# S5 branch of an encoder layer: products and sums moved from GpSimd to VectorE, plain copies moved to ScalarE

## Chip, cores and metric

The kernel runs on one core of one Trainium2 chip. The metric is the device time of one execution, in microseconds (us). Three executions of the kernel before took 2364.59, 2369.57 and 2371.45 us; their median is 2369.57 us.

## What is computed

One encoder layer on 1024 tokens of width 1024, in float32:

```
x = LN1(alpha*x + 0.5*SwiGLU_1(x))
x = LN2(alpha*x + W_out(g_A*W_oA(MLA(x)) + g_B*W_oB(S5(x))))
x = LN3(alpha*x + 0.5*SwiGLU_2(x))
x = LN4(alpha*x + sigmoid(x W_pg) * (p W_pp))
```

The change lies in the S5 branch, a bidirectional linear scan over 32 groups of 16 channels with 64 complex states each, once forward and once backward in time:

```
lam_bar = exp(lam*dt);  b_bar = ((lam_bar - 1)/lam) * b
bu = einsum(u, b_bar);  xs[t] = lam_bar*xs[t-1] + bu[t]     (or reversed)
y  = Re(einsum(xs, c)) forward + the same backward + d*u
z  = gelu(y);  S5 = z * sigmoid(z @ w_glu)
```

## The kernel before

TensorE computes float32 products as three products of a high and a low part each, so nearly every weight tile is first split: ScalarE copies the high part out (`split`, line 64), VectorE subtracts it from the raw tile (line 65). A slab of weights of 128 x 1024 takes 48 products of 128x512; the tiles of the high and low part have three buffers each.

The S5 branch (`s5_branch`, line 1032) is a generator. Its first part (to line 1247) makes tables from the parameters: powers of lam_bar (`PV`, `PW`), the tables `T1` and `T2` of the rotation angles, `br`, `bi` (b_bar) and the zeroed `bd` tiles. The tables T1 and T2 are made on GpSimd. Then come 8 steps, t = 0 to 7, of four groups each. Partitions 0 to 63 (`fw`) hold the forward direction, 64 to 127 (`bw`) the backward one.

- `gen(t)` (line 1249) makes the operands of step t: V = PV*c and W = PW*b_bar, both complex products of six 128x512 operations on VectorE (`cmul`, line 1139), with one more to negate the imaginary part of V (line 1263); four transposes each of W's parts (`pw`, line 1270) and their copies out of PSUM (`WTr`, `WTi`, line 1272); four copies of 64x64 into the block-diagonal `bd` (line 1278); the short kernel K from the products `pkx` (line 1283), which goes through DRAM into the Toeplitz tile M (lines 1292 and 1295); and C, S = T2*T1 (`Cw`, `Sw`, six operations on GpSimd, line 1298).
- `scan(t, ops)` (line 1302) makes the block sums `pe` on TensorE (line 1311), turns them by C and S (four products on VectorE, two sums on GpSimd), scans them over 128 blocks (`tensor_tensor_scan`, line 1327), and turns them back: four products on VectorE, then four half-width differences or sums, the forward halves on GpSimd (line 1335) and the backward halves, which are stored reversed, on VectorE (line 1336). The result is X, two tiles.
- `read_out(t, ops, X)` (line 1339) sums M, V and X into `py` on TensorE (lines 1344 and 1346), applies gelu (`zo`) and stores.

The main program calls the generator step by step (lines 767 to 773). Between two steps it issues two slabs of the projection that makes the gates (`project`, products `pg` at line 84), one slab after step 0. The program is placed by a scheduler that knows dependencies and estimated durations: it sets the order on each engine, so that products `pg` lie between the branch's own. Each engine works its own list in order. The projection of the latents with its root mean squares (`latents`, line 562, products `pms`) runs just ahead of step 0; part of it is on GpSimd (lines 591 to 594).

Of the kernel before, what the change touches and what calls it, by code (L numbers as in the profile page):

```python
# [24 lines left out]
AF = mybir.ActivationFunctionType  # L25
# [20 lines left out]
def layer_kernel(ctx, tc, A):  # L46
# [712 lines left out]
    sp = pool(left, "s5")  # L759
    s5p = pool(left, "s5p")  # L760
    step = s5_branch(tc, A, ud, zd, sp, s5p, dram, pdn, idt)
    next(step)
    project(sp, us[:2], state)
# [268 lines left out]
def s5_branch(tc, A, ud, zd, keep, pool, dram, pdn, idt):  # L1032
# [11 lines left out]
    V, S, G, PE = nc.vector, nc.scalar, nc.gpsimd, nc.tensor  # L1044
    MUL, ADD, SUB = ALU.mult, ALU.add, ALU.subtract

    def tile(shape, tag, bufs=1, dt=F32):
        return pool.tile([128] + shape, dt, tag=tag, bufs=bufs, name=tag)

    def load(name, shape):  # L1050
        t = tile(shape, name)
        nc.sync.dma_start(t, A[name])
        return t
# [3 lines left out]
    def t32(name):  # L1057
        if name not in slots:
            if not room:
                t = tile([16, 32], ("t2", "t3", "Xr")[len(slots) // 16])  # L1060
                room.extend(t[:, i, :] for i in range(16))
            slots[name] = room.pop()
        return slots[name]

    def tt(out, a, b, op, eng=G):
        eng.tensor_tensor(out=out, in0=a, in1=b, op=op)

    def ts(out, a, s1, op0, s2=None, op1=None, eng=G):
        if op1 is None:
            eng.tensor_scalar(out=out, in0=a, scalar1=s1, scalar2=None, op0=op0)  # L1070
        else:
            eng.tensor_scalar(out=out, in0=a, scalar1=s1, scalar2=s2, op0=op0, op1=op1)
# [31 lines left out]
    q, r, p, z = t32("q"), t32("r"), t32("p"), t32("z")  # L1104
# [34 lines left out]
    def cmul(outr, outi, a, b, tmp, eng=G):  # L1139
        tt(outr, a[0], b[0], MUL, eng)  # L1140
        tt(tmp, a[1], b[1], MUL, eng)
        tt(outr, outr, tmp, SUB, eng)
        tt(outi, a[0], b[1], MUL, eng)
        tt(tmp, a[1], b[0], MUL, eng)
        tt(outi, outi, tmp, ADD, eng)

    cr, ci = load("c_re", [32, 16]), load("c_im", [32, 16])
    br, bi = tile([32, 16], "bb_re"), tile([32, 16], "bb_im")
    PV = [tile([32, 8], f"PV{i}") for i in range(2)]
    PW = [tile([32, 8], f"PW{i}") for i in range(2)]  # L1150
    T1, T2 = (tile([32, 16], "T1r"), tile([32, 16], "T1i")), (tile([32, 8], "T2r"), tile([32, 8], "T2i"))
# [38 lines left out]
    def tmp(n, eng=G):  # L1190
        return bigs[eng][:, :, 0:n]

    rb = (tile([32, 16], "Vr", 2), tile([32, 16], "Vi", 2))
    nc.sync.dma_start(rb[0], A["b_re"])
    nc.sync.dma_start(rb[1], A["b_im"])
# [12 lines left out]
    fw, bw = slice(0, 64), slice(64, 128)  # L1208
# [40 lines left out]
    def gen(t):  # L1249

        ss = slice(4 * t, 4 * t + 4)
        B4 = [128, 4, 8, 16]

        def x(a):
            return a[:, ss, :, None].to_broadcast(B4)

        def y(a):
            return a[:, ss, None, :].to_broadcast(B4)

        g1, g2 = tile([4, 8, 16], "v1"), tile([4, 8, 16], "v2")  # L1260
        Vr, Vi = tile([4, 8, 16], "Vr", 2), tile([4, 8, 16], "Vi", 2)
        cmul(Vr, Vi, (x(PV[0]), x(PV[1])), (y(cr), y(ci)), g1, V)
        V.tensor_scalar(out=Vi, in0=Vi, scalar1=-1.0, scalar2=None, op0=MUL)
        Wr, Wi = tile([4, 8, 16], "Wr"), tile([4, 8, 16], "Wi")
        cmul(Wr, Wi, (x(PW[0]), x(PW[1])), (y(br), y(bi)), g1, V)
        WT = []
        for w, tag in ((Wr, "WTr"), (Wi, "WTi")):
            ps = pdn.tile([128, 512], F32, tag="dn", name="pw")
            for s in range(4):
                PE.transpose(ps[:, s * 128:s * 128 + 128], w[:, s].rearrange("p a b -> p (a b)"), idt)  # L1270
            o = tile([4, 128], tag, 2)
            S.activation(o, ps.rearrange("p (s n) -> p s n", s=4), AF.Copy)
            WT.append(o)
        Vf = [v.rearrange("p s a b -> p s (a b)") for v in (Vr, Vi)]

        for src, o in zip((br, bi), bd):
            for d, r in enumerate((fw, bw)):
                V.tensor_copy(o[r, :, 64 * d:64 * d + 16], src[r, ss, :])
        bz = [o.rearrange("p g x -> p (g x)") for o in bd]
        pk = pdn.tile([128, 512], F32, tag="dn", name="pkx")  # L1280
        for g in range(4):
            for i in range(2):
                PE.matmul(pk[:, 0:128], lhsT=bz[i][:, 112 * g:112 * g + 128], rhs=Vf[i][:, g, :],
                          start=(g == 0 and i == 0), stop=(g == 3 and i == 1))
        K = tile([240], "K")
        S.activation(K[fw, 0:128], pk[bw, 0:128], AF.Copy)
        S.activation(K[fw, 128:240], pk[fw, 16:128], AF.Copy)
        c = slice(112, 128)
        tt(K[0:64, c], K[0:64, c], pk[0:64, 0:16], ADD, V)
        V.scalar_tensor_tensor(out=K[0:64, c], in0=eye[0:64, :], scalar=dsk[0:64, t:t + 1], in1=K[0:64, c],  # L1290
                               op0=MUL, op1=ADD)
        nc.sync.dma_start(kd[t], K[0:64, :])
        M = tile([4, 128], "M", 2)
        for i in range(8):
            nc.sync.dma_start(M[i * 16:i * 16 + 16],
                              kd[t].rearrange("(g c) e -> c g e", c=16)[:, :, (7 - i) * 16:(7 - i) * 16 + 128])
        C_, S_ = tile([4, 8, 16], "Cw"), tile([4, 8, 16], "Sw")
        cmul(C_, S_, (x(T2[0]), x(T2[1])), (y(T1[0]), y(T1[1])), g2, G)
        CS = [o.rearrange("p s a b -> p s (a b)") for o in (C_, S_)]
        return Vf, WT, M, CS  # L1300

    def scan(t, ops):
        Vf, WT, M, (C_, S_) = ops
        E = []
        for i in range(2):
            e = pdn.tile([128, 512], F32, tag="dn", name="pe")
            ev = e.rearrange("p (s n) -> p s n", s=4)
            for g in range(4):
                u = U[:, 4 * t + g, :]
                for d, r in enumerate((fw, bw)):  # L1310
                    PE.matmul(ev[r, g, :], lhsT=WT[i][:, g, r], rhs=u if d == 0 else u[:, ::-1],
                              start=True, stop=True)
            E.append(ev)
        t1, t2, t3, t4 = [tile([4, 128], f"t{i}") for i in range(4)]
        h, b = slice(1, 128), slice(0, 127)
        for o in (t1, t3):
            G.memset(o[:, :, 0], 0.0)
        tt(t1[:, :, h], E[0][:, :, b], C_[:, :, h], MUL, V)
        tt(t2[:, :, h], E[1][:, :, b], S_[:, :, h], MUL, V)
        tt(t1[:, :, h], t1[:, :, h], t2[:, :, h], ADD, G)  # L1320
        tt(t3[:, :, h], E[1][:, :, b], C_[:, :, h], MUL, V)
        tt(t4[:, :, h], E[0][:, :, b], S_[:, :, h], MUL, V)
        tt(t3[:, :, h], t3[:, :, h], t4[:, :, h], SUB, G)
        X = x1, x3 = tile([4, 128], "Xr"), tile([4, 128], "Xi")
        for o, d in ((x1, t1), (x3, t3)):
            for s in range(4):
                V.tensor_tensor_scan(out=o[:, s, :], data0=r8[:, 4 * t + s:4 * t + s + 1].to_broadcast([128, 128]),
                                     data1=d[:, s, :], initial=0.0, op0=MUL, op1=ADD)

        tt(t1, x1, C_, MUL, V)  # L1330
        tt(t2, x3, S_, MUL, V)
        tt(t3, x3, C_, MUL, V)
        tt(t4, x1, S_, MUL, V)
        for o, x, y, op in ((X[0], t1, t2, SUB), (X[1], t3, t4, ADD)):
            tt(o[fw], x[fw], y[fw], op, G)
            tt(o[bw, :, ::-1], x[bw], y[bw], op, V)
        return X

    def read_out(t, ops, X):
# [18 lines left out]
    for b in range(4):  # L1358
        for j in range(8):
            nc.sync.dma_start(U[j * 16:j * 16 + 16, 8 * b:8 * b + 8, :], uv[b, j])  # L1360
    ops = gen(0)
    for t in range(8):
        X = scan(t, ops)
        nxt = gen(t + 1) if t < 7 else None
        yield
        last = read_out(t, ops, X)
        ops = nxt
# [96 lines left out]
```

## Time and profile before

| | |
|---|---|
| median of three executions | 2369.57 us |
| profiled execution: its time | 2375.43 us |
| profiled execution: its span | 2373.6 us |
| mean granted TensorE clock | 0.982 of full speed |
| steps t = 0 to 7 of the S5 branch | about 800 to 1032 us of the span |

The profile has a page for the whole span and views of its trace. In all of them PE is TensorE, PEld its weight loads, DVE is VectorE, ACT ScalarE, POOL GpSimd and SP the queue that issues transfers. A tile stands without its buffer number; "py<-Xr,Vr" is an instruction that writes py from Xr and Vr. An instruction's idle time before it stands in brackets, with what released it. PEclk is the granted TensorE clock, where 1.00 is 2.4 GHz and 0.50 is 1.2 GHz. Matmul durations overlap: what counts is the distance between their starts.

### The profile page before, as it was taken

What the parts mean: (1) busy time and instruction counts of PE and PEld (TensorE: products, weight loads), DVE (VectorE), ACT (ScalarE), POOL (GpSimd) and SP (SyncE); (2) the same over time, 40 slices, a digit from 0 to 9 for tenths busy, and PEclk for the clock granted to TensorE, in tenths of its full rate; (3) what the DMA queues carried; (4) which work ended last, traced back from release to release, by engine and by line L of the source; (5) the groups of instructions that cost most, each with busy time, mean ns of one, the idle gap of its engine ahead of it and who ended that gap; (6) DMA issues with size and microseconds to landing.
All of it is one profiled execution on the core that took longest, in us unless ns stands there. A gap on an engine that the chain in (4) does not pass through costs nothing.

```text
span 2373.6 us, 28494 instructions
## 1 busy us (share of the span) xinstructions
PE 2280.4 (96%) x10784; PEld 1876.8 (79%) x10784; DVE 1586.0 (67%) x2388; ACT 938.4 (40%) x1344; POOL 390.2 (16%) x419
## 2 busy tenths in 40 slices
PE   8999999999989989998999999989999999999897
PEld 7888888777768778886888888778888888777686
DVE  7565646665667899948688876665655646664836
ACT  5333333333432322234477871234333333233525
POOL 0000000000009455515255542000000000000000
PEclk9999999999999989998999999989999999999999
DMA  4332323932234222344100025122323327622211
GB/s 158 109 106 94 123 77 124 358 120 91 97 133 151 95 65 91 114 157 182 52 10 26 29 113 190 36 80 76 124 86 107 115 92 266 235 94 98 90 40 72
DMA packets 103899, 265.63 MB, mean 112 GB/s; under 512 B 13264, under 2 KB 27856, under 8 KB 103760
## 3 DMA queue, kind: packets, MB, share of 16 engines
q1 hardware_dynamic: 103760, 263.80, 32.3%
q8 instruction: 85, 1.39, 0.2%
q14 instruction: 54, 0.44, 0.1%
HBM read 189.33 MB, written 74.42 MB: 111 GB/s over the span
## 4 chain that ended last, share of the span: by engine, by line
PE 83%; DVE 7%; DMA 4%; issue 2%; ACT 2%; POOL 1%; SPq 0%; DVEq 0%; ACTq 0%; POOLq 0%
PE px L232 18%; PE pg L84 11%; PE py L232 9%; PE pdy L412 8%; PE pd L412 7%; PE pz L232 5%; PE pd L84 3%; PE pgate L84 3%; PE ps L84 3%; PE pov L706 2%; PE pu L270 2%; PE pg L270 2%; PE tpp L693 2%; PE pya L84 2%; DMA w2w<-in_ffn_w_dram 2%
## 5 line engine op out<-in xcount | busy, mean ns | idle before, releaser
L65 DVE TENSOR_TENSOR wlo<-raw,whi 128x1024 fp32r<-128x1024 f32 (+4 forms) x116 | 145.0, 1255 | 68.8 <-ACT whi L64 66.1
L64 ACT ACTIVATE whi<-raw 128x1024 fp32r<-128x1024 f32 (+4 forms) x116 | 112.3, 974 | 187.0 <-PE pg L84 111.4
L84 PE MATMUL pg<-xhi,whi 128*128 128x512 f32 x416 | 164.1, 395 | 0.1
L84 PE MATMUL pg<-xlo,whi 128*128 128x512 f32 x416 | 163.6, 393 | 0.3 <-DVE t L1201 0.3
L84 PE MATMUL pg<-xhi,wlo 128*128 128x512 f32 x416 | 162.9, 392 | 0.0
L412 PE MATMUL pd<-wl,hh 128*128 128x512 f32 x352 | 142.9, 406 | 6.0 <-DVE wl L65 6.0
L412 PE MATMUL pd<-wh,hl 128*128 128x512 f32 x352 | 140.9, 404 | 0.0
L412 PE MATMUL pd<-wh,hh 128*128 128x512 f32 x352 | 123.6, 404 | 7.5 <-ACT hh L64 6.6
L64 ACT ACTIVATE wh<-w2w 128x1024 fp32r<-128x1024 f32 x56 | 59.3, 1058 | 168.2 <-PE pd L412 84.2
L1232 POOL MEMSET T1r<- 128x32 f32 x1 | 0.2, 160 | 652.9 <-DMA x1d<-acc 652.9
L232 PE MATMUL py<-tch,fhl 128*128 128x512 f32 x320 | 106.0, 392 | 0.0
L412 PE MATMUL pdy<-wl,hh 128*128 128x512 f32 x264 | 104.4, 395 | 0.0
L412 PE MATMUL pdy<-wh,hl 128*128 128x512 f32 x264 | 103.9, 395 | 0.0
L65 DVE TENSOR_TENSOR hl<-raw,hh 128x1024 fp32r<-128x1024 f32 x84 | 94.9, 1132 | 11.3 <-ACT hh L64 11.2
L412 PE MATMUL pdy<-wh,hh 128*128 128x512 f32 x264 | 100.0, 396 | 0.0
L232 PE MATMUL px<-td,thi 128*128 128x512 f32 x320 | 98.8, 390 | 0.0
L64 ACT ACTIVATE fhl<-raw 128x512 fp32r<-128x512 f32 x40 | 25.3, 633 | 179.9 <-PE px L232 177.3
L65 DVE TENSOR_TENSOR wl<-w2w,wh 128x1024 fp32r<-128x1024 f32 x56 | 68.4, 1221 | 39.1 <-ACT wh L64 38.9
L680 POOL TENSOR_SCALAR P<-P,sm 128x1024 f32<-128x1024 f32 x64 | 74.8, 1170 | 117.1 <-DVE sm L679 98.4
L65 DVE TENSOR_TENSOR pt<-tpp,pt 128x512 fp32r<-128x512 f32 x128 | 85.6, 684 | 11.7 <-ACT pt L64 10.3
L84 PEld LDWEIGHTS pg<-xhi,whi 128*128 128x128 f32 x416 | 78.5, 189 | 17.2 <-issue 1.0
L84 PEld LDWEIGHTS pg<-xlo,whi 128*128 128x128 f32 x416 | 78.6, 189 | 16.8 <-DVE xlo L65 0.8
(431 smaller groups left out, 6395.0 us busy)
## 6 DMA issues: line engine op xcount, KB each, us to landing
raw<-in_ffn_w_dram SPq DMA_DIRECT2D x86, 512.0 KB, 3.7
raw<-hd SPq DMA_DIRECT2D x70, 512.0 KB, 3.3
hd<-c SPq DMA_DIRECT2D x88, 256.0 KB, 3.6
w2w<-in_ffn_w_dram SPq DMA_DIRECT2D x32, 512.0 KB, 8.6
hd<-s SPq DMA_DIRECT2D x60, 256.0 KB, 3.3
rawx<-in_xT_dram SPq DMA_DIRECT2D x16, 256.0 KB, 6.4
w2e<-in_ffn_w_dram SPq DMA_DIRECT2D x8, 512.0 KB, 8.8
acc<-in_x_dram SPq DMA_DIRECT2D x8, 512.0 KB, 8.8
```

The source lines that it names most:

```text
L64: S.activation(hi, src, AF.Copy)
L65: V.tensor_tensor(out=lo, in0=src, in1=hi.bitcast(F32), op=ALU.subtract)
L84: PE.matmul(out, lhsT=a, rhs=b, start=(n == 0), stop=(n == last))
L232: PE.matmul(out, lhsT=x[:, ks], rhs=y[:, k, :], start=(first and n == 0), stop=(n == 11), skip_group_check=True)
L270: PE.matmul(o, lhsT=x[:, ks], rhs=b[y][:, k, :], start=(i == 0 and k == 0 and m == 0), stop=(i == 1 and k == 3 and m == 2), skip_group_che ...
L412: PE.matmul(P[t], lhsT=x[:, ts], rhs=y[:, ws], start=(fresh and p + a == 0 and m == 0), stop=(p + a == NP - 1 and m == 2), skip_group_chec ...
L680: G.tensor_scalar(out=P, in0=P, scalar1=sm, scalar2=1.0, op0=ALU.mult, op1=ALU.mult)
L693: PE.transpose(tp[:, k * 128:k * 128 + 128], P[:, (q * 4 + k) * 128:(q * 4 + k) * 128 + 128], idt)
L706: PE.matmul(p[:, 0:256], lhsT=vt[:, k, c0:c0 + 128], rhs=pt[k // 4][b][:, k % 4, :], start=(k == 0 and b == 0), stop=(k == 7 and b == 1))
L1232: G.memset(T[0][:, :, 0], 1.0)
```

## The change

On VectorE and at full width of 128 partitions now stand the six operations for C and S, the two sums before the scan, and the two differences or sums after it. The halves of X are then written by four ScalarE copies of 64x512, two of them reversed. The four copies into `bd` are ScalarE copies, too. The negation of V's imaginary part is folded into the products: a table `cn` = -c_im is made once, and Vi = x0*cn - x1*cr. GpSimd keeps the tables, the root mean squares and, in the steps, two small memsets each.

```diff
@@ s5_branch
+    cn = tile([32, 16], "c_in")
+    ts(cn, ci, -1.0, MUL, eng=V)
     rb = (tile([32, 16], "Vr", 2), tile([32, 16], "Vi", 2))
@@ gen
-        cmul(Vr, Vi, (x(PV[0]), x(PV[1])), (y(cr), y(ci)), g1, V)
-        V.tensor_scalar(out=Vi, in0=Vi, scalar1=-1.0, scalar2=None, op0=MUL)
+
+        tt(Vr, x(PV[0]), y(cr), MUL, V)
+        tt(g1, x(PV[1]), y(ci), MUL, V)
+        tt(Vr, Vr, g1, SUB, V)
+        tt(Vi, x(PV[0]), y(cn), MUL, V)
+        tt(g1, x(PV[1]), y(cr), MUL, V)
+        tt(Vi, Vi, g1, SUB, V)
@@
-                V.tensor_copy(o[r, :, 64 * d:64 * d + 16], src[r, ss, :])
+                S.activation(o[r, :, 64 * d:64 * d + 16], src[r, ss, :], AF.Copy)
@@
-        cmul(C_, S_, (x(T2[0]), x(T2[1])), (y(T1[0]), y(T1[1])), g2, G)
+        cmul(C_, S_, (x(T2[0]), x(T2[1])), (y(T1[0]), y(T1[1])), g2, V)
@@ scan
-        tt(t1[:, :, h], t1[:, :, h], t2[:, :, h], ADD, G)
+        tt(t1[:, :, h], t1[:, :, h], t2[:, :, h], ADD, V)
@@
-        tt(t3[:, :, h], t3[:, :, h], t4[:, :, h], SUB, G)
+        tt(t3[:, :, h], t3[:, :, h], t4[:, :, h], SUB, V)
@@
         for o, x, y, op in ((X[0], t1, t2, SUB), (X[1], t3, t4, ADD)):
-            tt(o[fw], x[fw], y[fw], op, G)
-            tt(o[bw, :, ::-1], x[bw], y[bw], op, V)
+            tt(x, x, y, op, V)
+            S.activation(o[fw], x[fw], AF.Copy)
+            S.activation(o[bw, :, ::-1], x[bw], AF.Copy)
```

The first place is VectorE's list while the tables are still being made, ahead of step 0. Rows with Cw, Sw, T1 and T2 belong to the first C and S; wlo is the low part of a slab, line 579 sums squares for the latents. Before:

```order
L1066 TENSOR_TENSOR Vi<-Vi,v_5824 128x512
L1263 TENSOR_SCALAR Vi<-Vi 128x512
L1066 TENSOR_TENSOR v_5824<-PW_4779,bb_im 128x512
L65 TENSOR_TENSOR wlo<-raw,whi 128x1024 x2
L579 TENSOR_TENSOR rt_5229<-rt_5229,rt_5349 128x512
```

In the changed kernel the same place reads:

```order
L1066 TENSOR_TENSOR Vi<-Vi,v_5827 128x512
L1066 TENSOR_TENSOR v_5827<-PW_4779,bb_im 128x512
L1066 TENSOR_TENSOR Cw<-T2r,T1r 128x512
L1066 TENSOR_TENSOR Sw<-T2r,T1i 128x512
L65 TENSOR_TENSOR wlo<-raw,whi 128x1024
L1066 TENSOR_TENSOR v_5710<-T2i,T1i 128x512
L1066 TENSOR_TENSOR Cw<-Cw,v_5710 128x512
L1066 TENSOR_TENSOR v_5710<-T2i,T1r 128x512
L1066 TENSOR_TENSOR Sw<-Sw,v_5710 128x512
L1066 TENSOR_TENSOR v_5828<-T2i,T1i 128x512
L65 TENSOR_TENSOR wlo<-raw,whi 128x1024
L579 TENSOR_TENSOR rt_5231<-rt_5231,rt_5351 128x512
```

Two slabs' low parts and the sums for the latents now stand behind products of T1 and T2, which GpSimd writes.

The second place is VectorE's list at the end of the scan of step 0, between the last products that turn the result back and the short kernel K of gen(1). Before:

```order
L1066 TENSOR_TENSOR t_5795<-Xi,Sw 128x512
L1066 TENSOR_TENSOR t_5796<-Xi,Cw 128x512
L65 TENSOR_TENSOR wlo<-raw,whi 128x1024
L1066 TENSOR_TENSOR Wi<-PW_4778,bb_im 128x512
L1066 TENSOR_TENSOR Xr<-t_5794,t_5795 64x4x128
L1066 TENSOR_TENSOR Xi<-t_5796,t_5797 64x4x128
L1278 COPY bdr<-bb_re 64x4x16 x2
L1278 COPY bdi<-bb_im 64x4x16 x2
L1066 TENSOR_TENSOR K<-K,pkx 64x16
```

In the changed kernel:

```order
L1066 TENSOR_TENSOR Wi<-PW_4778,bb_im 128x512
L65 TENSOR_TENSOR wlo<-raw,whi 128x1024
L1066 TENSOR_TENSOR t_5796<-Xi,Sw 128x512
L1066 TENSOR_TENSOR t_5797<-Xi,Cw 128x512
L1066 TENSOR_TENSOR K<-K,pkx 64x16
L1066 TENSOR_TENSOR t_5795<-t_5795,t_5796 128x512
L1066 TENSOR_TENSOR Sw<-T2r,T1i 128x512
L1066 TENSOR_TENSOR t_5797<-t_5797,t_5798 128x512
L1066 TENSOR_TENSOR Cw<-T2r,T1r 128x512
```

X is no longer written there; the full-width differences stand in its place, with C and S of the next step between them, and the copies into bd are gone from this list.

The third place is ScalarE's list in a later step, from the copy out of line 452 to the gelu of the step. Before:

```order
L1272 ACTIVATE WTr<-pw 128x512
L64 ACTIVATE whi<-raw 128x1024
L452 ACT_TABLE_LOAD
L452 ACTIVATE og<-pg 128x1024
L1272 ACTIVATE WTi<-pw 128x512
L1286 ACTIVATE K<-pkx 64x128
L1287 ACTIVATE K<-pkx 64x112
```

In the changed kernel:

```order
L1343 ACTIVATE Xi<-t_6510 64x512
L1344 ACTIVATE Xi<-t_6510 64x4x128
L64 ACTIVATE whi<-raw 128x1024
L452 ACTIVATE og<-pg 128x1024
L1279 ACTIVATE WTi<-pw 128x512
L1285 ACTIVATE bdr<-bb_re 64x4x16 x2
L1293 ACTIVATE K<-pkx 64x128
L1294 ACTIVATE K<-pkx 64x112
L1285 ACTIVATE bdi<-bb_im 64x4x16 x2
```

The copies of X stand ahead of the next slab's high part, and the copies into bd around K.

## Rows read from the trace of the kernel before

**Rows 1.** The page: busy time, share of the span, instructions; GpSimd's slices
```profile
PE 2280.4 (96%) x10784; PEld 1876.8 (79%) x10784; DVE 1586.0 (67%) x2388; ACT 938.4 (40%) x1344; POOL 390.2 (16%) x419
...
POOL 0000000000009455515255542000000000000000
```

**Rows 2.** Windows: length, busy by engine, clock, transfers' share, GB/s
```profile
815.31:836.35 21.04, 16.16 (x108) 13.59 (x108) 20.87 (x30) 6.27 (x8) 13.38 (x11) 0.92 0.25 78
...
853.00:871.07 18.07, 12.26 (x86) 10.76 (x84) 14.60 (x20) 5.42 (x8) 7.75 (x8) 0.72 0.20 66
...
929.73:959.06 29.33, 29.33 (x178) 25.07 (x177) 29.13 (x40) 8.84 (x11) 15.94 (x12) 1.00 0.30 93
```

**Rows 3.** Timeline of TensorE, steps 0 to 2 and 7: start, duration, instruction
```profile
807.58 0.50 PE L84 MATMUL pg<-xhi,whi 128*128 128x512 f32 x1
...
830.79 0.46 PE L1346 MATMUL py<-Xr,Vr 128*128 128x128 f32 x2 [2.94 <-DVE Xr L1066]
...
858.45 1.11 PE L1270 MATMUL pw<-idt,Wr 128*128 128x128 f32 x4 [5.05 <-DVE Wr L1066]
...
871.07 0.50 PE L84 MATMUL pg<-xlo,whi 128*128 128x512 f32 x1
...
1029.15 0.46 PE L1346 MATMUL py<-Xi,Vi 128*128 128x128 f32 x2 [0.73 <-DVE Xi L1066]
```

**Rows 4.** The chain that ended last, one step's stretch: start, length, what
```profile
928.89 10.43 PE pg L84 x45
...
958.22 1.81 PE pg L84 x7
```

**Rows 5.** Groups of TensorE, 807.5 to 871 us: count, busy, mean ns
```profile
L84 PE MATMUL pg<-xhi,whi 128*128 128x512 f32 x46 | 18.3, 397 | 0.0
```

**Rows 6.** Groups of VectorE by shape, 871 to 1000 us
```profile
L1066 DVE TENSOR_TENSOR Xr<-t,t 64x512 f32<-64x512 f32 x4 | 10.7, 2681 | 0.1
L1066 DVE TENSOR_TENSOR Wr<-PW,bb_re 128x512 f32<-128x512 f32 x4 | 7.1, 1777 | 0.0
...
L1263 DVE TENSOR_SCALAR Vi<-Vi 128x512 f32<-128x512 f32 x5 | 7.0, 1391 | 0.2
...
L1066 DVE TENSOR_TENSOR v<-PV,c_im 128x512 f32<-128x512 f32 x4 | 5.7, 1436 | 0.1
L1278 DVE COPY bdr<-bb_re 64x64 f32<-64x64 f32 x8 | 4.9, 617 | 0.1
...
L1066 DVE TENSOR_TENSOR Vr<-PV,c_re 128x512 f32<-128x512 f32 x4 | 2.7, 676 | 0.0
```

**Rows 7.** Timeline of VectorE, a stretch in which GpSimd is mostly idle
```profile
897.23 1.21 DVE L65 TENSOR_TENSOR wlo<-raw,whi 128x1024 fp32r<-128x1024 f32 x1
898.36 0.68 DVE L1066 TENSOR_TENSOR Vr<-PV,c_re 128x512 f32<-128x512 f32 x1
898.97 0.68 DVE L1066 TENSOR_TENSOR Vi<-PV,c_im 128x512 f32<-128x512 f32 x1
...
906.49 1.36 DVE L1327 TENSOR_TENSOR_SCAN Xr<-r,t 128x128 f32<-128x128 f32 x4
907.77 0.66 DVE L1066 TENSOR_TENSOR Wr<-Wr,v 128x512 f32<-128x512 f32 x1
```

**Rows 8.** Timeline of ScalarE: copies like the new ones in size
```profile
782.59 0.64 ACT L577 ACTIVATE rt<-og 128x512 f32<-128x512 f32 x1 [3.22 <-POOL rt L592]
...
888.66 0.27 ACT L1286 ACTIVATE K<-pkx 64x128 f32<-64x128 f32 x1 [1.24 <-PE pkx L1283]
```

**Rows 9.** Timeline of GpSimd: the table T2
```profile
760.90 0.45 POOL L1066 TENSOR_TENSOR T2r<-T2r,v 128x128 f32<-128x128 f32 x1
```

**Rows 10.** Timeline of VectorE in step 0: copies into bd, last half of X
```profile
810.38 1.99 DVE L1278 COPY bdr<-bb_re 64x64 f32<-64x64 f32 x2
...
830.56 1.77 DVE L1066 TENSOR_TENSOR Xi<-t,t 64x512 f32<-64x512 f32 x1
```

**Rows 11.** Timeline of TensorE: first product of the latents' squares
```profile
774.18 0.39 PE L584 MATMUL pms<-rt,ones 128*128 128x512 f32 x1
```

## The prediction

> **What bounds the kernel now.** The page comes first: TensorE is busy for 96% of the span, VectorE for 67%, GpSimd for 16% [rows 1]. So only time that TensorE loses can be won back. GpSimd's slices place its work between about 710 and 1420 us; the branch's steps, 800 to 1032 us, are the part that the change touches.
>
> The windows of that part come second. In a later step, 929.73 to 959.06 us, TensorE is busy for all of 29.33 us at full clock [rows 2]. VectorE is busy for 29.13 of the same 29.33 us, but no wait of TensorE stands there: this step is as long as TensorE's own work. The two windows in steps 0 to 2 differ: 16.16 of 21.04 us busy at a clock of 0.92, then 12.26 of 18.07 us at 0.72 [rows 2].
>
> The timeline of TensorE says who is late: 2.94 us for X at 830.79, 5.05 us for W at 858.45, 0.73 us for X at 1029.15; VectorE is named each time [rows 3].
>
> How much is lost there is counted. In the steady step 45 products `pg` took 10.43 us, 0.232 each; from one such piece's start to the next step's is 958.22 - 928.89 = 29.33 us [rows 4]. A step has 96 products `pg` in TensorE's list, so 22.3 us, and 7.0 us are the branch's own. From the first `pg` behind `pe` of step 0 (807.58) to the first behind `pe` of step 2 (871.07) lie 63.49 us [rows 3]. In it stand 136 products `pg` (three groups of 46, 45 and 45 [rows 5]) and two sets of the branch's own: 136 x 0.232 + 2 x 7.0 = 45.6 us. TensorE loses 17.9 us there: 4.9 + 5.8 = 10.7 us idle by the two windows, and the rest, about 7 us, by work at the lower clock level: 0.92 and 0.72 are means of stretches at 2.4 and, behind the waits, at 1.2 GHz [rows 2]. With 0.7 us at 1029 the most that the change can win is 18.6 us.
>
> **The change part by part.**
>
> VectorE's price without GpSimd. In the steady step the same form, 128x512 out of SBUF, takes 676 ns for Vr<-PV,c_re and 1436 or 1777 ns for v<-PV,c_im and Wr<-PW,bb_re [rows 6]. The long ones lie where GpSimd works, the short ones where it rests; a half-width reversed sum took 2681 ns. In the quiet stretch two such operations start 0.61 us apart, a group of four scans is done 1.28 us after it began, a low part after 1.13 us [rows 7]. I take 0.60 us for each operation of 128x512 or 128x508.
>
> A changed step on VectorE then has 6 + 6 + 6 operations for V, W and C, S, 4 + 2 turns and sums before the scans, 4 + 2 after: 30 x 0.60 = 18.0 us; scans 2.56, two low parts 2.3, K 0.4: 23.3 us, against 29.13 before. New are the six for C and S and two sums, two full-width ones take the place of two half-width ones, and the negation (1391 ns) and four copies (two at 617 ns) go [rows 6]. In the steady step this wins nothing, since TensorE has no gap to close; 6 us of slack are left.
>
> The Trainium skill (GPSIMD Engine Reference, Specifications) says why both prices exist: GpSimd shares its SBUF interfaces with VectorE, and VectorE operations with two SBUF inputs contend. The trace agrees by 676 against 1777 ns. By that rule alone the added operations cost the short price once GpSimd rests, and the 23.3 us stand; without it the long price would be the operations' own, which is the last rival below.
>
> Step 0. GpSimd still works on the latents' root mean squares for some 3 us of it, so I cost two operations at 0.8 us more. At 810.38 VectorE's copies into bd began [rows 10]; they are gone, and K follows at once. From there to the first full difference stand 17 operations, 8 scans, one low part and three small ones: 10.2 + 2.56 + 1.13 + 0.45 + 1.6 = 15.9 us, so it ends at 826.3 and the second, two operations on, at 827.5. ScalarE then copies four halves. Its copy of 128x512 took 0.64 us [rows 8]; the reversed form is not in this trace. Bounds: 0.27 us, a 64x128 copy [rows 8], and 2.68, the reversed half on VectorE under contention [rows 6]. I take 0.64, the same length on the same engine. X's first tile is whole at 827.6, its second at 828.8. Before, the last half began at 830.56 and took 1.77 us, so it ended at 832.3 [rows 10]. TensorE's changed list asks for the first after 68 `pg` and the branch's own work but for most of `py`: 807.58 + 15.8 + (7.0 - 2.3) = 828.1, for the second four `pg`, 0.9 us, later. Both come in time, with 0.2 to 0.5 us to spare. At the upper bound of 2.68 TensorE would wait some 4 us.
>
> Step 1, the 5.05 us. The list has 29 operations, 8 scans, a low part and K between X's last difference and the end of Wr of gen(2): 17.4 + 2.56 + 1.13 + 0.15 = 21.2 us, done at 848.7. TensorE asks for it behind the rest of `py` and 82 `pg`: 828.1 + 0.9 + 2.3 + 19.0 = 850.3. In time by 1.6 us, up to 0.65 us per operation. The wait goes, and with it the low clock. Next in line is Wi, three operations and a low part on, with the same slack.
>
> The table place. VectorE now waits for T2r, which GpSimd ends at 760.90 + 0.45 = 761.35 [rows 9]. Behind that wait stand two low parts and the latents' sums of squares, which lead to `pms` on TensorE at 774.18 [rows 11]. The first low part belongs to the slab in which `pms` stands behind some 33 products, so it is needed at 774.18 - 33 x 0.232 = 766.5; behind two operations of 0.60 it is done at 763.7. Five operations and a low part more end at 767.8, two sums at 769.0, another low part at 770.2, the first of the last sums at 770.8; ScalarE has its high part at 771.4, 2.8 us ahead of `pms`. I cost this at nothing. If GpSimd were later, each us beyond the 2.8 would be one of TensorE's, once.
>
> ScalarE. Four halves at 0.64 and four copies of 64x64 at 0.27 or less make 3.6 us more per step; it is busy for 8.84 of 29.33 us [rows 2], so there is room. At 2.68 per reversed half it is 7.7 us, still covered. The copies of X stand ahead of a slab's high part; that slab is needed two slabs later.
>
> The last step. Behind the last `pe` VectorE runs ten operations and the scans, 8.6 us, and ScalarE 1.3; TensorE has 48 `pg`, 11.1 us. The 0.73 us go.
>
> Sum: 17.9 + 0.7 - 1.6 kept back for the two places with under 2 us to spare, X and W, = 17.0 us. The profiled execution was 2375.43 us, so it would be 2358.4; the median shown is 5.86 us lower, which gives 2352.6, rounded to 2353. What follows the branch starts earlier by the same amount: its transfers and waits hang on the last step and the last gate.
>
> **The rivals.**
>
> Half of it. The slack in steps 0 and 1 is a count of some 50 operations; at 0.65 us each with a reversed copy over 1 us, X or W stays 2 to 3 us late, the clock falls again behind the wait, and half of the 17.9 us remains. For it: under 0.5 us of slack at X. Against it: VectorE's idle rest grows after step 1. It gives 2369.6 - 9 = 2361.
>
> Nothing. The branch ends sooner, but what follows takes it back, or the table place moves the wait ahead of step 0: `pms` late by several us, then all that follows. For it: VectorE stands idle there with other work behind the wait. Against it: the slack of 2.8 us. It gives 2369.
>
> Slower: VectorE becomes the bound of the steady step. Its place is each of six steps. If the long price is the operations' own (strided or broadcast inputs), 26 of the 30 cost 1.35 us and the step 26 x 1.35 + 4 x 0.60 + 2.56 + 2.3 + 0.4 = 42.8 us against 29.33, 6 x 13.4 = 81 us more: 2450. It decides from (29.33 - 7.7) / 26 = 0.83 us per operation; at 0.9 it is +11 us, 2380. For it: VectorE is full today. Against it: identical forms at both prices in one step.
>
> **How the numbers follow.** Forecast 0.62, half 0.17, nothing 0.13, slower 0.08. The likeliest case's own range is 14 to 19 us won, 2350 to 2356. The range reaches to the half case and allows 3 us for the median's spread: 2347 to 2364. A difference below 0.3% (7.1 us) cannot be told from none here: faster 0.78, same 0.14, slower 0.08.
>
> **What would show it.** Right: a GpSimd nearly empty from 814 us to the end of the steps; no operation of 128x512 above 0.8 us on VectorE there, which is busy for about 23 of 29.3 us in a step; no wait of TensorE for Xr at step 0 nor for Wr at step 2, clock 1.00 from 800 to 1032 us, and that stretch about 17 us shorter; ScalarE near 12.4 us per step. Wrong: reversed copies above 1.5 us, a wait of `pw` for VectorE in each step, or a new wait of `pms` for VectorE near 775 us.

## The result, and the profile after

The changed kernel took 2347.66 us (median of four runs, 2342.87 to 2349.81) against 2367.93 for the kernel before in the same rounds: a ratio of 0.9911, 95% interval 0.9889 to 0.9933. The forecast was 2353, with 17.0 us won; about 21 us are won. Measured once more, the medians of five and of seventeen runs were 2348.11 and 2369.54 us, ratio 0.9916 (0.9903 to 0.9929), so 21.4 us.

The page after, in answer to [rows 1]: VectorE is busy for 40 us less although it has 25 more instructions, and GpSimd's slices are empty where the steps are.

```profile
PE 2270.6 (97%) x10784; PEld 1870.6 (80%) x10784; DVE 1545.7 (66%) x2413; ACT 966.5 (41%) x1408; POOL 267.0 (11%) x339
...
POOL 0000000000009300014355532000000000000000
```

Windows after, columns as in [rows 2]: from among the last `py` of step 0 to W of gen(2), and one later step.

```profile
829.00:848.75 19.75, 19.75 (x94) 16.46 (x93) 19.75 (x36) 8.47 (x10) 0.21 (x2) 1.00 0.33 106
939.05:968.37 29.32, 29.32 (x177) 25.07 (x177) 23.55 (x43) 12.38 (x20) 0.21 (x2) 1.00 0.38 114
```

TensorE has no gap and the full clock in both, and the later step is as long as before, 29.32 against 29.33 us. In it VectorE is busy for 23.55 us (worked out: 23.3) and ScalarE for 12.38 (12.4).

Groups by shape after, 870 to 1000 us, VectorE and then ScalarE, in answer to [rows 6, 8]:

```profile
L1066 DVE TENSOR_TENSOR t<-t,t 128x512 f32<-128x512 f32 x10 | 6.8, 682 | 0.0
L1066 DVE TENSOR_TENSOR v<-PV,c_im 128x512 f32<-128x512 f32 x4 | 2.7, 683 | 0.0
L1066 DVE TENSOR_TENSOR Wr<-PW,bb_re 128x512 f32<-128x512 f32 x4 | 2.7, 682 | 0.0
...
L1344 ACT ACTIVATE Xi<-t 64x512 f32<-64x512 f32 x5 | 3.1, 629 | 0.1
L1285 ACT ACTIVATE bdr<-bb_re 64x64 f32<-64x64 f32 x8 | 2.0, 255 | 4.1 <-PE pkx L1290 4.0
```

Both long forms of [rows 6], 1436 and 1777 ns, are at 682 to 683 with the same operands. The reversed copy on ScalarE takes 629 ns. The two places of [rows 3] after, TensorE: no bracket with a wait stands behind them. The third and fourth row bound the branch, its first `pw` and last `py`; the fifth and sixth are the same two before.

```profile
826.73 0.39 PE L1354 MATMUL py<-Xr,Vr 128*128 128x128 f32 x2
...
848.75 0.60 PE L1277 MATMUL pw<-idt,Wr 128*128 128x128 f32 x4
...
798.67 0.60 PE L1277 MATMUL pw<-idt,Wr 128*128 128x128 f32 x4
...
1011.10 0.39 PE L1354 MATMUL py<-Xi,Vi 128*128 128x128 f32 x2
```

```profile
800.17 0.60 PE L1270 MATMUL pw<-idt,Wr 128*128 128x128 f32 x4
...
1031.24 0.39 PE L1346 MATMUL py<-Xi,Vi 128*128 128x128 f32 x2
```

That is 231.1 us before and 212.4 after, from row to row; the table below counts to the second product of the last row, and so gives 212.5. Cut at the starts of such products, the two profiles of each kernel (the second from the experiments) read, in us:

| stretch | before | after | difference |
|---|---|---|---|
| first `pms` to first `pw` | 26.0, 26.0 | 26.0, 25.9 | 0 |
| first `pw` to last `py`: the branch | 231.1, 231.1 | 212.5, 212.6 | -18.6 |
| last `py` to first `pglu` (gate of the S5 output) | 21.9, 21.9 | 21.9, 21.9 | 0 |
| first `pglu` to first `pk` (keys of attention) | 23.1, 23.5 | 21.2, 21.3 | -2.0 |
| first `pk` to first `tpp` (attention) | 84.5, 80.7 | 81.9, 83.9 | spread |
| first `tpp` to last `pgate` | 1198.4, 1195.2 | 1198.5, 1195.2 | spread |
| last `pgate` to the end | 14.4, 14.5 | 13.3, 13.3 | -1.1 |

The three differences that recur in both profiles are 21.7 us together.

### The profile page after: what moved, and what is told of

It reads as the page before. It is cut to its first block, busy times and chain, and to the rows that moved or that the text cites. A ratio compares the mean times of both kernels' runs of the same rounds, so it can differ in the third digit from the quotient of the medians.

```text
span 2348.0 us, 28499 instructions
## 1 busy us (share of the span) xinstructions
PE 2270.6 (97%) x10784; PEld 1870.6 (80%) x10784; DVE 1545.7 (66%) x2413; ACT 966.5 (41%) x1408; POOL 267.0 (11%) x339
## 4 chain that ended last, share of the span: by engine, by line
PE 86%; DVE 6%; DMA 4%; ACT 2%; issue 1%; SPq 0%; POOL 0%; DVEq 0%; ACTq 0%
PE px L232 18%; PE pg L84 12%; PE py L232 9%; PE pdy L412 8%; PE pd L412 7%; PE pz L232 5%; PE pd L84 3%; PE pgate L84 3%; PE ps L84 3%; PE pov L706 2%; PE pu L270 2%; PE pg L270 2%; PE tpp L693 2%; PE pya L84 2%; DMA w2w<-in_ffn_w_dram 2%; PE pyb L84 2%
## 5 line engine op out<-in xcount | busy, mean ns | idle before, releaser
L84 PEld LDWEIGHTS pg<-xlo,whi 128*128 128x128 f32 x416 | 78.4, 189 | 16.5 <-DVE xlo L65 0.8
L84 PEld LDWEIGHTS pg<-xhi,wlo 128*128 128x128 f32 x416 | 78.3, 188 | 16.6 <-issue 0.3
L246 DVE TENSOR_TENSOR c<-raw 128x512 f32<-128x512 f32 x40 | 27.5, 688 | 94.0 <-PE px L232 93.9
```

The source lines that it names most:

```text
L84: PE.matmul(out, lhsT=a, rhs=b, start=(n == 0), stop=(n == last))
L246: V.tensor_tensor(out=c[:, r], in0=r2[:, l], in1=r2[:, r], op=ALU.add)
```

## Experiments

**The two kernels once more.** No edit.

> The changed kernel once more, as it stands. In the two profiles so far the branch itself ended 18.6 us sooner, and the stretch behind it, from the first product of the S5 gate (pglu) to the first transpose of attention (tpp), was 107.6 us long before and 103.1 us after; the sum said this stretch would not change. Theory A (the stretch is shorter whenever the branch ends sooner): about 103 us again, and the ratio to the kernel before near 0.990. Rival B (it is spread from one execution to the next): a length anywhere between 103 and 108 us, and a ratio near 0.992, which is the branch's 18.6 us alone.

> The kernel before once more, as it stands: its ratio to itself says what these rounds can tell from no change (0.998 to 1.002 expected). Theory A of the stretch behind the branch: pglu to tpp about 107.6 us again. Rival B: anywhere between 103 and 108 us.

Measured: ratios 0.9916 (0.9903 to 0.9929) for the changed kernel and 0.9996 (0.9986 to 1.0006) for the kernel before. `pglu` to `tpp` was 105.2 us after and 104.2 before: as a whole it is spread from one execution to the next, as B has it. But its first piece recurs, and the trace shows what goes with it. GpSimd's scaling of the latents (line 821) and VectorE's product with the gate (line 812) start within a microsecond of each other. GpSimd and VectorE, before and then after:

```profile
1068.46 13.78 POOL L821 TENSOR_TENSOR lat<-lat,rms 128x1024 f32<-128x1024 f32 x5 [40.00 <-DMA lat<-latd]
...
1068.83 5.68 DVE L812 TENSOR_TENSOR sg<-sg,zT 128x512 f32<-128x512 f32 x2
```

```profile
1049.23 14.06 POOL L821 TENSOR_TENSOR lat<-lat,rms 128x1024 f32<-128x1024 f32 x5 [63.27 <-DMA lat<-latd]
...
1048.70 3.50 DVE L812 TENSOR_TENSOR sg<-sg,zT 128x512 f32<-128x512 f32 x2
```

Where GpSimd starts first, both of VectorE's operations are long (5.68 us for the two); where VectorE starts first, only the second is (3.50 us). In all eleven profiles in which line 821 is on GpSimd the stretch goes with this order: GpSimd is first in both of before and in three of the experiments below (C and S, the halves of X, the sums), VectorE in the other six. `pglu` to `pk` is 23.0 to 23.5 us in the one case and 21.1 to 21.3 in the other. In the five of the first case, and in none of the six, TensorE waits for mx, as here with the sums on GpSimd:

```profile
PE pk L84 <- ACT mx L822: 1.7, 1, 1.7
```

So it is a race, in which a load releases one side and the margin is 0.04 to 0.53 us. The edit touches neither line. Yet both profiles of each kernel fell the same way, and no run shows whether the edit sets who wins.

The Trainium skill (SBUF — State Buffer, SBUF: two separate sides) calls the port pair of the two engines a lock that whichever starts first holds for its whole instruction. The eleven profiles agree, by 5.68 against 3.50 us.

**GpSimd busy, nobody waiting for it.**

```diff
         cmul(C_, S_, (x(T2[0]), x(T2[1])), (y(T1[0]), y(T1[1])), g2, V)
+        idle = tile([4, 128], "idle")
+        for _ in range(10 if t else 0):
+            tt(idle, WT[0], WT[1], MUL, G)
...
-            G.memset(o[:, :, 0], 0.0)
+            V.memset(o[:, :, 0], 0.0)
```

> The changed kernel, with ten products of 128x512 per step added on GpSimd from gen(1) on, which nobody reads (as many as stood there before), and the two small memsets of the scan on VectorE, so that no other engine waits for GpSimd in the steps. Theory (VectorE's long prices come from GpSimd working beside it): before, a step on VectorE was some 9.7 us longer than its operations at the short price, with ten GpSimd operations beside it, so 1 us per GpSimd operation; the changed step of 23.3 us becomes about 33 us against TensorE's 29.33. Waits of TensorE for VectorE come back in steps 1 and 2 and then stand in every step: 6 x 3.7 = 22 us, and some 13 us in steps 0 to 2, so about 2383 us (2365 to 2395), slower than the kernel before. Rival (the change won because VectorE and TensorE no longer wait for results that GpSimd makes, not because operations became shorter): no difference, 2348 us, VectorE's 128x512 operations at 0.68 us.

Measured: 2380.86 us, 1.0051 (1.0039 to 1.0063) of the kernel before, close to the theory's 2383; the branch 244.5 us, 32 more than after. TensorE's waits for VectorE and ScalarE are back, 23.9 us of them, mostly for W (us in total, times, longest):

```profile
PE pw L1277 <- DVE Wr L1066: 16.7, 4, 7.4
```

No wait of TensorE, VectorE or ScalarE in the branch names GpSimd. VectorE's timeline in a later step, and then GpSimd's:

```profile
915.66 0.67 DVE L1066 TENSOR_TENSOR v<-PV,c_im 128x512 f32<-128x512 f32 x1
916.28 0.67 DVE L1066 TENSOR_TENSOR v<-T2i,T1r 128x512 f32<-128x512 f32 x1
...
916.98 1.66 DVE L1066 TENSOR_TENSOR Sw<-Sw,v 128x512 f32<-128x512 f32 x1
918.68 1.65 DVE L1066 TENSOR_TENSOR v<-T2i,T1i 128x512 f32<-128x512 f32 x1
920.26 2.29 DVE L65 TENSOR_TENSOR wlo<-raw,whi 128x1024 fp32r<-128x1024 f32 x1
```

```profile
901.90 16.19 POOL L1066 TENSOR_TENSOR idle<-WTr,WTi 128x512 f32<-128x512 f32 x1
...
918.18 1.61 POOL L1066 TENSOR_TENSOR idle<-WTr,WTi 128x512 f32<-128x512 f32 x1
```

One product of GpSimd stands for 16.19 us while VectorE's run at 0.67 without a gap; once it is through, the two take turns, and each of VectorE's is about 1 us longer. So the long price needs no result of GpSimd that anybody waits for, and here it is paid by the engine that comes second.

**C and S back on GpSimd.**

```diff
-        cmul(C_, S_, (x(T2[0]), x(T2[1])), (y(T1[0]), y(T1[1])), g2, V)
+        cmul(C_, S_, (x(T2[0]), x(T2[1])), (y(T1[0]), y(T1[1])), g2, G)
```

> The changed kernel with the six operations for C and S back on GpSimd. So far the branch, from the first pw to the last py, took 231.1 us in both profiles of the kernel before and 212.5 in those of the changed one; with ten idle products per step on GpSimd 244.5, so about 1 us of VectorE's time for each GpSimd product. Theory (each GpSimd product costs VectorE about 1 us): a step on VectorE is 23.55 - 3.6 + 6 = 26 us, still under TensorE's 29.33, so no wait in the later steps; in steps 0 to 2 VectorE is up to 2 x 2.4 us later against some 2 us of slack, so waits of 0 to 6 us in all. Branch 213 to 219 us, time about 2351. Rival (C and S are the part that brought the gain): branch about 230 us, time 2366.

Measured: 2354.78 us, 0.9928 (0.9905 to 0.9951); branch 219.3 us, just above the theory's end of 219. Its mechanism was half wrong. From 900 to 1000 us:

```profile
900.00:950.00 50.00, 50.00 (x315) 42.99 (x314) 34.30 (x55) 23.88 (x38) 23.02 (x16) 1.00 0.35 106
950.00:1000.00 50.00, 50.00 (x281) 42.48 (x280) 33.03 (x60) 19.88 (x30) 22.00 (x15) 1.00 0.36 110
```

VectorE is busy for 67.33 of 100 us, 19.7 per step, not 26: it lost six operations and pays nothing for GpSimd's six; that they pass in VectorE's idle time is the likely reason, which no run tries by itself. The loss is in steps 0 to 2, where TensorE waits 3.3 us for W. One more wait stands there, VectorE's for the memset on GpSimd, queued behind its products:

```profile
DVE t L1066 <- POOL t L1324: 2.4, 1, 2.4
```

**C and S alone moved, in the kernel before.** The opposite edit, in the kernel before.

> The kernel before with one part of the change: the six operations for C and S on VectorE; sums, halves of X, negation and bd copies as before. Theory (1 us per GpSimd product): four products per step remain on GpSimd; a step on VectorE goes from 29.13 to 29.13 + 3.6 - 6 = 26.7 us. In steps 0 to 2 the gain is about two thirds of the whole one, since the four that remain lie in the chain from pe to X. Branch 215 to 222 us, time about 2355 to 2360. Rival (the sums and halves in the chain to X are what counts): branch 228 to 231, time 2366 to 2370.

Measured: 2358.68 us, 0.9949 (0.993 to 0.9968); branch 224.5 us, 6.6 less than before. That is a third of the gain, between the two forecasts: of TensorE's waits in the branch, 11.6 us before, 9 us stay, the longest 3.7 for Wr.

**The halves of X as before.**

```diff
-            tt(x, x, y, op, V)
-            S.activation(o[fw], x[fw], AF.Copy)
-            S.activation(o[bw, :, ::-1], x[bw], AF.Copy)
+            tt(o[fw], x[fw], y[fw], op, G)
+            tt(o[bw, :, ::-1], x[bw], y[bw], op, V)
```

> The changed kernel with the halves of X as before: forward halves on GpSimd, backward halves, reversed, on VectorE, no copies on ScalarE. Theory: two products per step on GpSimd beside two half-width ones on VectorE, so VectorE's step is some 2 us longer at 25.5 us, no wait in the later steps; at step 0 X, which was ready 1.5 us ahead, is about 2 us later: TensorE waits 0 to 2 us, and the W of gen(2), ready 2.1 us ahead, is 0 to 2 us late. Branch 212.5 to 216 us, time 2348 to 2351. Rival (writing the reversed halves directly, 2681 ns in the trace of before, was a cost of its own): more than 2 us per step on VectorE even without GpSimd's company, and branch above 217 us.

Measured: 2352.54 us, 0.9913 (0.9895 to 0.9932); branch 216.1 us, the theory's end. The rival is out: the reversed half of Xi took VectorE 0.69 us (median of eight), so writing it reversed has no long price of its own. W is late by 2.1 us, X by 0.3:

```profile
PE pw L1277 <- DVE Wr L1066: 2.1, 1, 2.1
PE py L1353 <- DVE Xi L1066: 0.3, 1, 0.3
```

**bd copies and negation back on VectorE.**

```diff
-        tt(Vi, x(PV[0]), y(cn), MUL, V)
+        tt(Vi, x(PV[0]), y(ci), MUL, V)
...
-        tt(Vi, Vi, g1, SUB, V)
+        tt(Vi, Vi, g1, ADD, V)
+        V.tensor_scalar(out=Vi, in0=Vi, scalar1=-1.0, scalar2=None, op0=MUL)
...
-                S.activation(o[r, :, 64 * d:64 * d + 16], src[r, ss, :], AF.Copy)
+                V.tensor_copy(o[r, :, 64 * d:64 * d + 16], src[r, ss, :])
```

> The changed kernel with two small parts undone: the four copies into bd and the negation of V's imaginary part are VectorE's again. One operation of 0.6 us and four of about 0.15 more per step: 1.2 us. Theory (what counts is GpSimd's company, and VectorE has over 2 us of slack at the two places that were late): nothing, branch 212.5 us, the copies at 0.1 to 0.2 us each in place of 0.62, time 2348. Rival (the shorter list of VectorE is what brought the gain): branch 214 to 218 us, time 2350 to 2354.

Measured: 2350.9 us, 0.9913 (0.9897 to 0.9929); branch 214.3 us, as the rival had it, though the copies took 0.19 us, as the theory had it. Neither X nor W is late, but the short kernel's way through DRAM is:

```profile
PE py L1353 <- DMA M<-kd: 1.2, 1, 1.2
```

**The two sums before the scan back on GpSimd.**

```diff
-        tt(t1[:, :, h], t1[:, :, h], t2[:, :, h], ADD, V)
+        tt(t1[:, :, h], t1[:, :, h], t2[:, :, h], ADD, G)
...
-        tt(t3[:, :, h], t3[:, :, h], t4[:, :, h], SUB, V)
+        tt(t3[:, :, h], t3[:, :, h], t4[:, :, h], SUB, G)
```

> The changed kernel with the two sums before the scan back on GpSimd, the last part not yet undone. So far, undone one at a time, C and S cost the branch 6.8 us, the halves of X 3.6, bd and negation 1.8: 12.2 of the 18.6. Theory A (the parts add up): 6.4 us are left for the sums, branch about 219 us, time about 2354. Theory B (the parts share one slack of about 2 us at X and W, so that each costs only what goes beyond it): two products per step cost as much as the two halves of X, 2 to 4 us, branch 214.5 to 216.5, time about 2350 to 2352.

Measured: 2352.12 us, 0.9939 (0.9925 to 0.9952); branch 214.4 us, 1.9 more than after; X is late by 1.2 us. The four parts undone alone cost 6.8 + 3.6 + 1.8 + 1.9 = 14.1 us, less than the 18.6 of all together, which fits theory B: they share one slack. Two things limit this. Each branch length is from one profile, and by their times the kernels with the halves and with the bd copies undone (0.9913 each) can't be told from the changed one (0.9916). And the scheduler places every kernel anew: from the first `pw` to the first product with X it is 28.1 us in the changed kernel, 26.4 with the halves as before and 30.8 with the bd copies back, so a part of each cost can be the new order.

**VectorE given more work.**

```diff
+        idle = tile([4, 8, 16], "idle")
+        for _ in range(14 if t > 2 else 0):
+            tt(idle, Vr, Vi, MUL, V)
```

> The changed kernel with 14 products of 128x512 added to each step's operands from gen(3) on, on VectorE, which nobody reads. VectorE was busy for 23.55 of 29.33 us in a step, so room for 5.8 us or nine such operations. Theory (TensorE's own work sets the step until VectorE passes it): 23.55 + 14 x 0.60 = 32 us per step, 2.6 us over, five times, less the lead of up to 5.8 us that VectorE has at first: 7 to 13 us more, branch 220 to 226 us, time 2355 to 2361; TensorE waits for VectorE in the later steps and nowhere in steps 0 to 2. Rival (VectorE's idle time in a step is bound up in waits for other engines and can't be used): 5 x 8.4 = 42 us more, 2390.

Measured: 2369.24 us, 1.0012 (1.0003 to 1.0021); branch 232.4 us, 19.9 more than after. VectorE is busy for 49.12 and 49.44 us of each 50 from 900 to 1000 us, so its room can be used: the rival's 42 us are out. TensorE does not wait in steps 0 to 2 nor anywhere in the branch before 1000 us. But the price is above the theory's 7 to 13 us: from 1000 us on, waits of 15.8 us come within 32 us, and the granted clock there is 0.79. Why they come together at the end was not tried.

TensorE's waits there (line, what it waited for: us in total, times, longest):

```profile
PE py L1357 <- ACT Xr L1347: 5.7, 1, 5.7
PE pw L1277 <- DVE Wi L1066: 5.0, 1, 5.0
PE py L1355 <- DMA zd<-zo: 4.6, 1, 4.6
PE py L1357 <- ACT Xi L1347: 0.5, 1, 0.5
```

**The latents' scaling on VectorE.**

```diff
-            G.tensor_tensor(out=lat[i], in0=lat[i], in1=rstd[i], op=ALU.mult)
+            V.tensor_tensor(out=lat[i], in0=lat[i], in1=rstd[i], op=ALU.mult)
```

> The changed kernel, with the five products of 128x1024 by which the latents are scaled (line 821) on VectorE in place of GpSimd. In the profile after they take 2.8 us each there while VectorE's 128x512 operations beside them take 1.7 to 2.8 us in place of 0.68, and TensorE waits 6.2 us for the low part of the latents (ckl). Theory (the same contention sits in this stage): the five cost VectorE 1.2 us each, the operations beside them fall to 0.68 us, the wait of 6.2 us goes to under 2 us, and the time is 4 to 6 us below the changed kernel's, about 2343 us. Rival (the loads of the latents set this stage, or VectorE gets 6 us more on the same path): no difference, 2348 us, with TensorE's wait at 5 to 7 us.

Measured: 2339.03 us, 0.9876 (0.9863 to 0.9888), 9 us below the changed kernel, more than theory or rival gave. In the changed kernel TensorE waits there:

```profile
PE pk L84 <- DVE ckl L823: 6.2, 1, 6.2
```

Windows from the first `pk` to the first `pyb`, the changed kernel and then this one:

```profile
1054.30:1070.80 16.50, 10.30 (x33) 7.86 (x32) 16.50 (x12) 8.35 (x11) 9.93 (x5) 0.79 0.13 40
```

```profile
1050.90:1056.90 6.00, 6.00 (x28) 4.69 (x26) 6.00 (x7) 4.40 (x6) 0.00 (x0) 1.00 0.12 29
```

The 6.20 us of TensorE's wait for ckl are gone, the low clock behind it too, and a few products moved behind; from `pglu` to `tpp` 7.3 us remain won against the first profile of the changed kernel (9.4 against its second). The forecast of 4 to 6 us had left out the clock.

**Three more of GpSimd's operations on VectorE, with the latents' scaling.**

```diff
-        G.tensor_tensor(out=kr, in0=kr, in1=tab, op=ALU.mult)
+        V.tensor_tensor(out=kr, in0=kr, in1=tab, op=ALU.mult)
...
-            G.tensor_tensor(out=t[b], in0=t[b], in1=tab[b, sl], op=ALU.mult)
+            V.tensor_tensor(out=t[b], in0=t[b], in1=tab[b, sl], op=ALU.mult)
...
-            G.tensor_tensor(out=ql[r], in0=t[r], in1=qh[r].bitcast(F32), op=ALU.subtract)
+            V.tensor_tensor(out=ql[r], in0=t[r], in1=qh[r].bitcast(F32), op=ALU.subtract)
```

> The changed kernel with the latents' scaling on VectorE (which took 2339.0 us, 0.9876 of the kernel before) and three more GpSimd operations of the stage behind it there too: the product of the key's and of the queries' rows with the rope table (lines 608 and 658) and the low part of the queries (line 661). Beside them in the last trace VectorE's operations of 32x1024 took 2.2 us in place of about 1.2, and TensorE waited 2.6 and 0.8 us for gb, with a clock of 0.93 in the 20 us around it. Theory (contention again): the wait of 2.6 us goes and with it the low clock, 2 to 4 us less, 2335 to 2337 us. Rival (VectorE gets these operations on the path to gb, so that the wait stays): no difference, 2338 to 2340 us.

Measured: 2360.88 us, 0.9971 (0.9961 to 0.998), far from both forecasts. `pglu` to `tpp` fell to 93.5 us, but `tpp` to `pgate` rose to 1218.3, since the last two lines run for every head of attention. VectorE's largest group there, 1130 to 1330 us, with the latents alone moved and then here:

```profile
L65 DVE TENSOR_TENSOR pt<-tpp,pt 128x512 fp32r<-128x512 f32 x95 | 63.7, 684 | 5.9 <-ACT pt L64 5.0
```

```profile
L65 DVE TENSOR_TENSOR pt<-tpp,pt 128x512 fp32r<-128x512 f32 x88 | 58.5, 683 | 2.6 <-ACT pt L64 1.8
```

It was at its short price all along, in the first of the two beside a GpSimd busy for 109 of those 200 us: here nothing was to be won, and VectorE got two more operations, of 0.73 and 0.89 us, for each half of a head's queries. From 1126 to 1420 us TensorE's waits for VectorE rose from 5.1 to 20.7 us. The Trainium skill (GPSIMD Engine Reference, Specifications) has the two engines contend when VectorE reads two inputs out of SBUF; here one of them, `tpp`, lies in PSUM, and the 684 ns agree.

**The same for the first two heads alone.** Lines 658 and 661 with `(V if hd < 2 else G)`, line 608 as above.

> As the kernel with the latents' scaling on VectorE (2339.0 us), with the key's rope product (line 608) and, for the first two heads alone, lines 658 and 661 on VectorE as well; the later heads, whose moves cost 20 us in attention (tpp to gate 1218.3 in place of 1197.9 us), keep them on GpSimd. Theory (the loss came from the later heads, where VectorE's operations were at their short price all along): tpp to gate is 1198 us again, pglu to tpp stays at the 93.5 us reached there against 95.8, and the time is 2336 to 2338 us, 2 us below the kernel with the latents alone. Rival (the 2 us are spread): 2339 to 2341.

Measured: 2340.38 us, 0.9876 (0.9854 to 0.9897). `tpp` to `pgate` is 1197.9 us again and `pglu` to `tpp` 93.4, so the loss did come from the later heads; the 2 us won ahead of attention can't be told from none in the time.

## Why the prediction was too careful

- **What bounds the kernel, and VectorE's price without GpSimd: right.** VectorE's operations start 0.60 us apart, its step is 23.55 us, and with idle products on GpSimd the long price came back without anybody reading them.
- **Steps 0 and 1: right, with more slack than argued.** VectorE's second difference ended at 825.1 us; 827.5 was worked out for a profile whose branch began 1.5 us later, so it was 0.9 us sooner. X's first tile was whole at 825.25, 1.5 us ahead of TensorE (0.5 worked out), and its second at 826.55; Wr of gen(2) was done at 846.65, 2.1 us ahead (1.6 worked out).
- **The table place: right.** VectorE waited 13.85 us for T2r, and `pms` stood at 772.68 without a wait (774.18 before, where the whole of the span up to here was 1.5 us later).

```profile
757.27 0.73 DVE L1066 TENSOR_TENSOR Cw<-T2r,T1r 128x512 f32<-128x512 f32 x1 [13.85 <-POOL T2r L1066]
```

- **ScalarE and the last step: right.** The reversed copy is no dearer than a plain one, and TensorE waits nowhere for X.
- **The sum: wrong in two terms.** It gave 17.0 us where 21.4 were measured. "17.9 + 0.7 - 1.6 kept back": the 18.6 us, of which idle time and low clock were counted one by one, came whole in both profiles, so nothing was to be kept back. And "What follows the branch starts earlier by the same amount" put the stretches behind the branch at nothing: they gave 3.1 us more. 2.0 us came with the race of line 821 with line 812, in which GpSimd was first in both profiles of the kernel before, and 1.1 us from the end of the span. Of the latter the rows show where it lies, not why: the last VectorE pair ends 4.17 us ahead of the end of the span before (2373.6 - 2368.02 - 1.41), 3.03 after (2348.0 - 2343.56 - 1.41). Before, and again in its second profile, one transfer of instructions stands among those of the last 9 us (queue, kind: packets, MB, share of 16 engines); after, none does. It is the same in all fourteen profiles: 14.4 and 14.5 us from the last `pgate` to the end in the two with such a transfer, 13.3 or 13.4 in the twelve without, among them the kernel before with C and S alone moved. That the transfer is the cause was not tried.

```profile
2368.02 1.41 DVE L133 SCALAR_TENSOR_TENSOR acc<-acc,ln,ln 128x512 f32<-128x512 f32 x2
```

```profile
q14 instruction: 1, 0.01, 0.2%
```

```profile
2343.56 1.41 DVE L133 SCALAR_TENSOR_TENSOR acc<-acc,ln,ln 128x512 f32<-128x512 f32 x2
```

- **The rivals.** Half and nothing are excluded by the branch's 212.5 us. The slower one needs a long price of the operations' own; they have none. VectorE as the bound exists, but only with more work: 14 operations more in a step brought it there, fewer were not tried.

## What to carry to other kernels

Where an engine shows the same form of operation at two prices, and the change empties the engine beside which the long ones lie, compute with the short price. Then look for the same pair of engines in the stages behind: time can move there with who starts first, though the edit doesn't touch the stage. In this kernel, moving work from GpSimd to VectorE paid where VectorE's operations beside it were long and TensorE waited for them; where they were at their short price already, it only filled VectorE. And parts of a change are not priced one by one where they draw on the same slack, as they seem to here: undone alone they cost 14.1 us of 18.6.

## What the runs showed of the hardware

- A GpSimd product of 128x512 that came second stood for 16.19 us behind VectorE's unbroken run of short ones, against 1.05 us for GpSimd's first product for C in the kernel before (761.90 us), where VectorE was idle; and VectorE's took 1.66 in place of 0.67 us once the two took turns.
- A wait of TensorE cost more than its length: 11.6 us of waits in the kernel before went and the branch won 18.6; 15.8 us of waits with more work on VectorE cost it 19.9; taking 6.2 us away won 7.3 up to `tpp`. In the second case the granted clock was 0.79 on average over the 32 us with the waits, in the third over 16.5 us, a mean of 2.4 and, behind the wait, 1.2 GHz: behind the wait in the changed kernel, products `pk` start 0.43 us apart, and 0.23 some 5 us later.
